# Merging three branches by tokens instead of by features, in a decoder block on one Trainium2 core

## The chip, the core and the metric

The kernel runs on one core of one Trainium2 chip. A core has a matrix engine (TensorE, PE in the profile; its weight loads are listed apart as PEld), a vector engine (DVE), a scalar engine (ACT), GpSimd (POOL) and a queue that issues transfers (SP). Each engine works through its own list of instructions in order; engines wait for each other by semaphores. SBUF is the working memory with 128 partitions, PSUM the small memory into which PE writes its sums: eight banks of 512 float32 for each partition.

The metric is the time of one execution on the device in microseconds (us). Three runs of the kernel before took 562.88, 562.93 and 563.34 us; the median is 562.93.

## What is computed

One decoder block for 256 tokens of width 1024, in float32: a sandwich of RMS norms around three token mixers that run in parallel (a sparse attention "NSA" with 16 heads in 4 groups, an mLSTM with 4 heads, cross-attention to 256 memory tokens), a merge of the three by gates, an output projection with residual, and a SwiGLU channel mixer of width 2816. The part that matters here:

```python
gm = jax.nn.sigmoid(g_merge.reshape(B, S, N_BRANCH, D_MODEL))
y = (gm[:, :, 0] * (y_nsa @ w_proj_nsa[l]) + gm[:, :, 1] * (y_ml @ w_proj_ml[l])
     + gm[:, :, 2] * (y_mem @ w_proj_mem[l]))
x = x + rmsnorm(y @ w_out[l], g_post_mix[l])
h = rmsnorm(x, g_pre_ffn[l])
gu = h @ w_ffn_in[l]
```

`g_merge` is the last part, 3 x 1024 columns, of `z = h @ w_in`. `y_nsa` has 1024 features, `y_ml` and `y_mem` have 512 each.

## The kernel before

**Exact products.** A float32 operand is split in two float32r tiles, high and low part: ACT copies (rounds) into the high one, DVE subtracts it from the source into the low one (`split`, line 429). A product is then three matmuls: high x high, high x low, low x high (`mm3`, line 457). A matmul has a stationary operand of 128 x 128, and streams up to 512 columns of the other one.

**Weights.** All large weights come as a stream of 162 units of [128, 1024] float32 (512 KB), in the order in which they are used. `unit` (line 452) fetches the next one by a DMA on SP's queue into one of four `raw` buffers and splits it into `whi` and `wlo` (four buffers each); these are ACT's `whi<-raw` and DVE's `wlo<-raw,whi` of the profile.

**Two layouts of a product.** `fmaj` (line 462) makes 128 output features for 256 tokens: the weights are stationary, the 256 tokens stream by, 24 matmuls of 256 columns for a unit of 8 blocks. `fpair` (line 470) makes two such feature tiles side by side in one PSUM bank. `tmaj` (line 477) makes [128 tokens, 512 features] for both halves of the tokens, in two banks: the activations are stationary, 512 columns of the weights stream by, 12 matmuls of 512 columns for a unit, six for each token half. In the names of the profile both look alike, for instance `pd<-hh,whi` (by features, 256 columns) and `pd<-whi,hh` (by tokens, 512).

**PSUM.** Eight banks by tags: `d` 2 (dense products, `pd`), `s` 3 (scores; `pss`, `pnl`, `sc`), `t` 2 (transposes and small things), `v` 1 (attention values). `ps_ds` (line 418) takes two of five tiles from `d` and three from `s`, in turn.

**The plan.** The program is first recorded (`Plan.record`): every instruction with what it reads and writes. `schedule` (line 265) then runs a list schedule with modelled costs: on each engine the ready instruction that comes first in the program is next. Tiles of a tag get their buffers in program order, so that a tile waits until those recorded before it have theirs. `cost` (line 228) is the model; for a matmul it is the columns divided by 2.4 per ns, plus 2 ns. The order that comes out is what the engines get.

**The stages around the change.** The attention of NSA runs over four groups `g` and two token halves `tb` (`nsa_queries`, `nsa_half`). Its chain of scores, maximum, exponential, transposes and values is long, and other work is recorded between its parts: a string `ORDER` of tasks, of which `FILL` (line 28) takes so many after each half. The first twelve tasks are parts of the mLSTM (`q`, `s`, `g`, `v`, `h`, `f`), the others are `merge_pair` ("m"): one pair of the 24 feature tiles of the merge gates, copied raw into `gm[b]` of [128, 8, 256]. `gm` has features on the partitions, one tile for each branch.

After the last group comes the merge, a loop over 8 feature tiles: the projections of the mLSTM (`pl_`), the memory branch (`pm_`) and NSA (`pn_`) by `fmaj` from two units, three multiplies with the gates, two adds (`mrg`), and a split into `yh`, `yl`. The gates' sigmoids are taken in place, after the last exponentials (`after=last_exp`), so that ACT's table is changed only once. `yh` and `yl`, features on the partitions, are the stationary operands of the output projection (`scaled`, `tmaj` by tokens with `ps_ds`), whose sums are normed and added to the residual. The channel mixer then takes the last 190 us.

Of the kernel before, what the change touches and what calls it, by code (L numbers as in the profile page):

```python
# [10 lines left out]
F32 = mybir.dt.float32  # L11
F32R = mybir.dt.float32r
# [5 lines left out]
P = 128  # L18
S = 256          # tokens
D = 1024  # L20
KD = D // P      # feature tiles of the model dimension
# [6 lines left out]
FILL = (5, 7, 1, 2, 3, 1, 3, 2)  # L28
ORDER = "qqvqqsghhhhfmmmmmmmmmmmm"
# [3 lines left out]
# columns of w_in  # L33
C_Q, C_KV, C_G, C_ML, C_IF, C_O, C_QM, C_MG = 0, 1024, 2560, 2608, 4144, 4152, 4664, 5176

# columns of the array of constants
K_ID, K_TRI, K_RV, K_BM, K_M0, K_C1, K_MT, K_END = 0, 128, 256, 257, 261, 533, 549, 677
# columns of the array of gains and small weights
# [4 lines left out]
class View:  # L43
    """A part of a tile that has no place yet."""
# [54 lines left out]
    def region(self):  # L99
        """First and last partition, and the elements of a partition as bits."""  # L100
        t = self.tile
        key = repr(self.steps)
        if key not in t.regions:
            p = int(self.ix.flat[0]) // t.n
            bits = np.zeros(t.n, bool)
            bits[self.ix[0].ravel() % t.n] = True
            t.regions[key] = (p, p + self.shape[0], int.from_bytes(np.packbits(bits).tobytes(), "big"))
        return t.regions[key]


class Slot:
    """A tile of the plan: its place is chosen when its first instruction is issued."""
# [50 lines left out]
class Plan:  # L163
    """Records the instructions in program order, with what they read and write, and issues them
    in the order of a list schedule: on every engine the ready one that comes first in the
    program. Tiles of a tag get their buffers in program order."""
# [9 lines left out]
    def later(self, n):  # L176
        """The instructions inside come as if n places later in the program."""
# [50 lines left out]
    def cost(op):  # L228
# [7 lines left out]
        if op.eng == "PE":  # L236
# [3 lines left out]
            return n / rate + 2  # L240
# [24 lines left out]
    def schedule(self):  # L265
# [10 lines left out]
        def offer(op):  # L276
            """Makes op a candidate if its new tiles can have places; else it waits for the tag."""
# [10 lines left out]
        def held(op):  # L288
            """A bank of PSUM serves one engine at a time, and so do the ports that GpSimd shares."""
# [96 lines left out]
def block_kernel(ctx, tc, order, xN, xT, memT, cst, vec, row, wg, w1, w2, W, out):  # L386
# [75 lines left out]
    def fmaj(out, xs, ks, wu, b0=0, first=True, last=True):  # L462
        """out [128 features, 256] += blocks of a unit (from b0) times the tiles ks of xs."""
# [6 lines left out]
    def fpair(xs, w, i, ps_new=ps_d):  # L470
        """[128, 2, 256]: the i-th pair of feature tiles of the weights w."""
# [5 lines left out]
    def tmaj(xs, *key, n=4, ps_new=ps_d, into=None, last=0):  # L477
        """[128 tokens, 512] for both halves of the tokens, from n units of two feature tiles each; the
        last ones are used for the first half of the tokens before the second."""
# [29 lines left out]
    def warm_up(n):  # L509
        """Products of no use, that bring the tensor engine's clock up while it would wait."""  # L510
# [4 lines left out]
    def colsum(sq):  # L515
        """[128, 2]: per token, the sum of sq [128, 2, 256] over the partitions and the tiles."""
# [7 lines left out]
    def bcast(r, ps):  # L524
        """ps [128, 256]: the column r [128, 2] of the tokens, on every row."""
# [114 lines left out]
    msk = one.tile([P, 416], BF16, name="msk")          # m0 (272), c1 (16), mt (128)  # L640
# [56 lines left out]
    # running sums of logf, and i - sums  # L697
# [34 lines left out]
    # columns: selected keys 128-255, 0-127, compressed keys, window keys 0-127, 128-255  # L732
# [63 lines left out]
    for h2 in range(2):  # L796
        pvm = ps_v([P, 2, S], "pvm")
        ptm = [[work.tile([P, 2, S], F32R, tag=f"pT{i}", bufs=2, name="pTm") for i in range(2)] for _ in range(2)]
        for tb in range(2):
# [18 lines left out]
            pt = ps_t([P, 2, 2, P], "ptx")          # m tile, head, t  # L818
# [102 lines left out]
    gm = [bigt("G", 3, [P, 8, S], F32, f"gm{b}") for b in range(3)]  # L921

    def merge_pair(i):
        ps = fpair(X, "g_merge", i)
        ACT.activation(gm[i // 4][:, 2 * (i % 4):2 * (i % 4) + 2, :], ps, AF.Copy)
# [20 lines left out]
    def nsa_half(g, tb, qs, yT):  # L946
# [71 lines left out]
        for e in range(2):  # L1018
# [5 lines left out]
             "h": ml_head, "f": lambda _: ml_finish(), "m": merge_pair}  # L1024
# [16 lines left out]
    last_exp = exps[-12:]  # L1041

    def sigmoids(i):
        for b in range(3):
            g2 = gm[b][:, 2 * i:2 * i + 2, :]
            ACT.activation(g2, g2, AF.Sigmoid, after=last_exp)
# [3 lines left out]
    for fi in range(8):  # L1050
        ps = ps_s([P, 2, S], "pnl")
        pn_, pl_, pm_ = ps[:, 0, :], ps[:, 1, :], ps_t([P, S], "pmm")
        if fi % 2 == 0:
            sigmoids(fi // 2)
        w = unit(("proj", 2 * fi + 1))
        fmaj(pl_, yml, range(4), w)
# [221 lines left out]
```

## Time and profile before

| | |
|---|---|
| median of three runs | 562.93 us |
| span of the profiled execution | 561.4 us |
| attention with tasks between, from the first scores | about 111 to 298 us |
| projections of the branches and merge | 296 to 342 us |
| output projection and residual | 342 to 391 us |
| channel mixer | to the end |
| weight stream | 159 units of 512 KB and 6 half units, 51.5% of the DMA engines' time |

The span is that of one profiled execution, from its first to its last instruction; the page gives no other time of that execution. The profile shows an instruction of PE with a modelled end. PE overlaps the end of one matmul with the next: a 256-wide one is drawn some 0.28 us long and the next begins after 0.12 us. Line numbers do not help to tell instructions apart, since the plan issues all from line 382; the names of the tiles do.

### The profile page before, as it was taken

To read this page: it belongs to the slowest core of one execution; us is meant where nothing else is said; L and a number is where in the kernel's file an instruction comes from. 1 tells how busy PE (TensorE), PEld (TensorE's weight loads), DVE (VectorE), ACT (ScalarE), POOL (GpSimd) and SP (SyncE) were. 2 spreads that over 40 slices of the span, in tenths; PEclk is the share of its full clock that TensorE was granted. 3 is DMA by queue.
4 is the path that set the end of the run, shared out by engine and by line. 5 is a ranking of instruction groups with operands and counts; after the bars stand their busy time and mean duration, and the time that the engine had idled before them with its cause. 6 is when DMAs were issued, how large, how long until landed. Compare 5 with 4: busy or idle time off the path is not lost.

```text
span 561.4 us, 10304 instructions
## 1 busy us (share of the span) xinstructions
PE 551.9 (98%) x3964; PEld 516.5 (92%) x3964; DVE 404.5 (72%) x802; ACT 334.2 (60%) x658; POOL 36.0 (6%) x44
## 2 busy tenths in 40 slices
PE   8999999999999999999999999999999999999994
PEld 8899998998989999999999998878999999988883
DVE  4897398598897989987786877865565656654543
ACT  6775677566596858777697444774444444444430
POOL 1110000002002011302111000000000000000000
PEclk9999999999999999999999999999999999999998
DMA  7994327617345253434435655744555545556522
GB/s 246 356 350 154 113 86 228 205 56 238 129 121 180 76 178 124 135 119 160 151 117 158 216 189 188 257 156 123 177 189 183 182 175 179 186 185 191 189 71 75
DMA packets 29281, 95.28 MB, mean 170 GB/s; under 512 B 3376, under 2 KB 6704, under 8 KB 28976
## 3 DMA queue, kind: packets, MB, share of 16 engines
q1 hardware_dynamic: 29232, 94.63, 51.5%
q8 instruction: 31, 0.51, 0.4%
q14 instruction: 18, 0.15, 0.1%
HBM read 92.52 MB, written 1.05 MB: 167 GB/s over the span
## 4 chain that ended last, share of the span: by engine, by line
PE 92%; DMA 3%; ACT 2%; DVE 2%; issue 0%; SPq 0%; DVEq 0%; ACTq 0%
PE pd L382 46%; PE pss L382 23%; PE pnl L382 6%; PE sc L382 3%; PE pvn L382 3%; PE pmm L382 2%; PE ptn L382 2%; DMA memt<-in_memT 2%; PE ph L382 2%; ACT whi L382 1%; DMA raw<-in_W 1%; PE pw L382 1%; PE pn L382 1%; PE pgf L382 1%; PE psm L382 1%; PE pvm L382 1%
## 5 line engine op out<-in xcount | busy, mean ns | idle before, releaser
L382 DVE TENSOR_TENSOR wlo<-raw,whi 128x1024 fp32r<-128x1024 f32 (+1 forms) x161 | 195.4, 1217 | 102.1 <-ACT whi L382 100.7
L382 ACT ACTIVATE whi<-raw 128x1024 fp32r<-128x1024 f32 (+1 forms) x161 | 167.6, 1046 | 164.3 <-issue 72.3
L382 PE MATMUL pd<-hh,whi 128*128 128x256 f32 x416 | 119.7, 288 | 0.3 <-DVE vs L382 0.3
L382 PE MATMUL pd<-hh,wlo 128*128 128x256 f32 x416 | 119.7, 288 | 0.0
L382 PE MATMUL pd<-hl,whi 128*128 128x256 f32 x416 | 119.5, 287 | 0.0
L382 PEld LDWEIGHTS pd<-hh,whi 128*128 128x128 f32 x416 | 79.5, 191 | 0.8 <-DVE vs L382 0.7
L382 PEld LDWEIGHTS pd<-hl,whi 128*128 128x128 f32 x416 | 79.4, 191 | 0.1
L382 PEld LDWEIGHTS pd<-hh,wlo 128*128 128x128 f32 x416 | 79.4, 191 | 0.0
L382 PE MATMUL pss<-xh,wlo 128*128 128x256 f32 x160 | 45.4, 284 | 0.0
L382 PE MATMUL pss<-xl,whi 128*128 128x256 f32 x160 | 45.4, 284 | 0.0
L382 PE MATMUL pss<-xh,whi 128*128 128x256 f32 x160 | 45.4, 283 | 0.0
L382 PE MATMUL pss<-whi,u 128*128 128x512 f32 x132 | 42.4, 392 | 0.0
L382 PE MATMUL pd<-xh,whi 128*128 128x256 f32 x128 | 36.2, 283 | 0.0
L382 PE MATMUL pd<-xl,whi 128*128 128x256 f32 x128 | 36.2, 283 | 0.0
L382 PE MATMUL pd<-xh,wlo 128*128 128x256 f32 x128 | 36.2, 283 | 0.0
L382 PEld LDWEIGHTS pss<-xh,whi 128*128 128x128 f32 x160 | 30.7, 192 | 0.0
L382 PEld LDWEIGHTS pss<-xl,whi 128*128 128x128 f32 x160 | 30.7, 192 | 0.0
L382 PEld LDWEIGHTS pss<-xh,wlo 128*128 128x128 f32 x160 | 30.7, 192 | 0.0
L382 PEld LDWEIGHTS pss<-whi,u 128*128 128x128 f32 x132 | 24.8, 188 | 5.5
L382 ACT ACTIVATE pp<-sc,mx 128x128 f32<-128x128 f32 (+1 forms) x64 | 27.1, 439 | 0.4 <-DVE mx L382 0.3
L382 PE MATMUL pss<-wlo,u 128*128 128x512 f32 x66 | 25.9, 392 | 0.0
L382 DVE TENSOR_REDUCE mx<-sc 128x1 f32<-128x16 f32 (+2 forms) x96 | 22.6, 284 | 3.3 <-PE sc L382 3.0
(306 smaller groups left out, 1243.9 us busy)
## 6 DMA issues: line engine op xcount, KB each, us to landing
raw<-in_W SPq DMA_DIRECT2D x159, 512.0 KB, 3.4
w<-in_w SPq DMA_DIRECT2D x2, 1024.0 KB, 7.0
raw<-in_W SPq DMA_DIRECT2D x6, 256.0 KB, 5.6
xt<-in_xT SPq DMA_DIRECT2D x2, 512.0 KB, 7.6
x<-in_xN SPq DMA_DIRECT2D x2, 512.0 KB, 4.9
out<-z SPq DMA_DIRECT2D x8, 128.0 KB, 2.0
memt<-in_memT SPq DMA_DIRECT2D x6, 128.0 KB, 5.4
wgt<-in_wg SPq DMA_DIRECT2D x1, 512.0 KB, 6.3
```

Of the source, the lines that this page charges most:

```text
L382: op.ins_ = getattr(op.real, op.method)(*map(arg, op.a), **{k: arg(x) for k, x in op.kw.items()})
```

## The change

The gates and the branch projections are made by tokens. `gm[b]` becomes [128 tokens, 2, 1024]; `merge_half` makes 512 gates of a branch for all tokens from four units, six times in all, and copies them out by ACT. `ORDER` has six "m" in place of twelve, and `FILL` puts one after each of the last six attention halves. The merge becomes a loop over two halves `h` of the features: for the mLSTM, the memory branch and NSA in this order a sigmoid in place (1024 elements at once), the projections by `tmaj` in the banks of `ps_ds`, and for each half of the tokens a multiply (and an add for the second and third branch) into a [128, 1024] tile `mrg` of tag `p`, which has two buffers. Then PE transposes the sum, four tiles of 128 x 128 into one bank (`pty`), and ACT and DVE split it into `yh` and `yl`. The plan counts 13 ns in place of 2 for each float32r matmul besides its columns. The units hold other columns of the weights; there are as many as before. Comments are gone too; the diff leaves them out.

```diff
-FILL = (5, 7, 1, 2, 3, 1, 3, 2)
-ORDER = "qqvqqsghhhhfmmmmmmmmmmmm"
+FILL = (5, 7, 1, 1, 1, 1, 1, 1)
+ORDER = "qqvqqsghhhhfmmmmmm"
...
-            return n / rate + 2
+            return n / rate + (13 if dtype == F32R and op.method != "transpose" else 2)
...
-    gm = [bigt("G", 3, [P, 8, S], F32, f"gm{b}") for b in range(3)]
-
-    def merge_pair(i):
-        ps = fpair(X, "g_merge", i)
-        ACT.activation(gm[i // 4][:, 2 * (i % 4):2 * (i % 4) + 2, :], ps, AF.Copy)
+    gm = [bigt("G", 3, [P, 2, D], F32, f"gm{b}") for b in range(3)]
+
+    def merge_half(i):
+        b, h = i % 3, i // 3
+        for tb, ps in enumerate(tmaj(X, "g_merge", b, h)):
+            ACT.activation(gm[b][:, tb, 512 * h:512 * h + 512], ps, AF.Copy)
...
-             "h": ml_head, "f": lambda _: ml_finish(), "m": merge_pair}
+             "h": ml_head, "f": lambda _: ml_finish(), "m": merge_half}
...
     last_exp = exps[-12:]
-
-    def sigmoids(i):
-        for b in range(3):
-            g2 = gm[b][:, 2 * i:2 * i + 2, :]
-            ACT.activation(g2, g2, AF.Sigmoid, after=last_exp)
 
     yh = bigt("hh", 1, [P, 8, S], F32R, "yh")
     yl = bigt("hl", 1, [P, 8, S], F32R, "yl")
-    for fi in range(8):
-        ps = ps_s([P, 2, S], "pnl")
-        pn_, pl_, pm_ = ps[:, 0, :], ps[:, 1, :], ps_t([P, S], "pmm")
-        if fi % 2 == 0:
-            sigmoids(fi // 2)
-        w = unit(("proj", 2 * fi + 1))
-        fmaj(pl_, yml, range(4), w)
-        fmaj(pm_, ymem, range(4), w, 4)
-        fmaj(pn_, (ynh, ynl), range(8), unit(("proj", 2 * fi)))
-        m = work.tile([P, 3, S], F32, tag="p", bufs=2, name="mrg")
-        for b, x in enumerate((pn_, pl_, pm_)):
-            DVE.tensor_mul(m[:, b, :], x, gm[b][:, fi, :])
-        for b in (1, 2):
-            DVE.tensor_add(m[:, 0, :], m[:, 0, :], m[:, b, :])
-        split(yh[:, fi, :], yl[:, fi, :], m[:, 0, :])
+    for h in range(2):
+        c = slice(512 * h, 512 * h + 512)
+        m = [work.tile([P, 1024], F32, tag="p", bufs=2, name="mrg") for _ in range(2)]
+        for b, name, xs, n in ((1, "proj_ml", yml, 2), (2, "proj_mem", ymem, 2), (0, "proj_nsa", (ynh, ynl), 4)):
+            g2 = gm[b][:, :, c]
+            ACT.activation(g2, g2, AF.Sigmoid, after=last_exp)
+            for tb, ps in enumerate(tmaj(xs, name, h, n=n, ps_new=ps_ds)):
+                acc, new = m[tb][:, 0:512], m[tb][:, 512:1024]
+                if b == 1:
+                    DVE.tensor_mul(acc, ps, gm[b][:, tb, c])
+                else:
+                    DVE.tensor_mul(new, ps, gm[b][:, tb, c])
+                    DVE.tensor_add(acc, acc, new)
+        for tb in range(2):
+            pt = ps_t([P, 4, P], "pty")
+            for j in range(4):
+                PE.transpose(pt[:, j, :], m[tb][:, j * P:(j + 1) * P], ident)
+            t = slice(tb * P, (tb + 1) * P)
+            split(yh[:, 4 * h:4 * h + 4, t], yl[:, 4 * h:4 * h + 4, t], pt)
...
-    add_f("g_merge", w_in, tiles(C_MG, 24))
-    pn, pl, pm = a["w_proj_nsa"][0], a["w_proj_ml"][0], a["w_proj_mem"][0]
-    for i in range(8):
-        c = slice(i * P, (i + 1) * P)
-        units["proj", 2 * i] = blocks(pn, c).reshape(P, 1024)
-        units["proj", 2 * i + 1] = np.concatenate([blocks(pl, c), blocks(pm, c)], axis=1).reshape(P, 1024)
+    for b in range(3):
+        for h in range(2):
+            c = C_MG + 1024 * b + 512 * h
+            add_t("g_merge", w_in[:, c:c + 512], b, h)
     for h in range(2):
+        for b in ("nsa", "ml", "mem"):
+            add_t("proj_" + b, a["w_proj_" + b][0][:, 512 * h:512 * h + 512], h)
```

## The prediction, made before the changed kernel was run

> **What bounds the kernel now.** I read the page first: the busy table, the 40 slices and the chain that ended last.
>
> ```profile
> span 561.4 us, 10304 instructions
> PE 551.9 (98%) x3964; PEld 516.5 (92%) x3964; DVE 404.5 (72%) x802; ACT 334.2 (60%) x658; POOL 36.0 (6%) x44
> PE   8999999999999999999999999999999999999994
> PEclk9999999999999999999999999999999999999998
> PE 92%; DMA 3%; ACT 2%; DVE 2%; issue 0%; SPq 0%; DVEq 0%; ACTq 0%
> ```
>
> TensorE (PE) is busy in every slice but the first and the last, at full granted clock, and makes 92% of the chain. Busy time of pipelined matmuls proves little, so the next view is the busy time by stretches (columns: stretch, length, then PE with its count, weight loads, DVE, ACT, POOL, clock, DMA share, GB/s). I cut it at the stages: heads and selected attention with the merge gates' products between (100 to 293), branch projections (293 to 343), output projection (343 to 395).
>
> ```profile
> 60.00:100.00 40.00, 40.00 (x298) 37.98 (x297) 31.55 (x69) 28.47 (x59) 1.31 (x1) 1.00 0.50 148
> 100.00:135.00 35.00, 34.67 (x240) 31.37 (x238) 28.89 (x70) 20.17 (x49) 5.32 (x4) 1.00 0.47 147
> 135.00:195.00 60.00, 59.88 (x449) 55.30 (x450) 51.79 (x118) 46.83 (x112) 3.13 (x3) 1.00 0.44 141
> 195.00:293.00 98.00, 98.00 (x824) 95.89 (x823) 83.04 (x227) 71.63 (x194) 14.88 (x12) 1.00 0.43 141
> 293.00:343.00 50.00, 50.00 (x418) 49.91 (x417) 39.42 (x67) 26.38 (x37) 3.49 (x2) 1.00 0.57 180
> 343.00:366.00 23.00, 22.84 (x105) 18.77 (x105) 18.18 (x24) 15.04 (x25) 0.55 (x1) 1.00 0.70 233
> ```
>
> In the two stages that the change rewrites (195 to 343) PE never shows a gap, while DVE and ACT keep room. The same holds outside: from 60 to 366 PE's idle time adds up to 0.33 + 0.12 + 0.16 = 0.61 us. So what a changed instruction is worth there is what it holds PE, from start to start, and not the duration that its row shows. The starts come from the chain of waits in order of time (start, length, what, count):
>
> ```profile
> 305.24 4.31 PE pnl L382 x36
> 309.55 1.43 PE pmm L382 x12
> 395.73 11.52 PE pd L382 x96
> 543.50 5.44 PE pss L382 x24
> 548.94 5.45 PE pd L382 x24
> ```
>
> A 256-wide product in an unbroken run takes 11.52/96 = 120.0 ns; in the projections (4.31 + 1.43)/48 = 119.6 ns. A 512-wide product (548.94, the last projection) takes 5.45/24 = 227.1 ns. Two narrow ones cost 240, one wide one 227 for the same columns: 12.9 ns saved for each pair.
>
> **The change part by part.** *Gates.* `merge_pair` ran 12 times with 2 units of 8 x 3 narrow products, 576 x 120.0 ns = 69.1 us. `merge_half` runs 6 times with 4 units x 2 token halves x 2 x 3 wide ones, 288 x 227.1 = 65.4 us. That is 3.7 us off PE. Weights, their splits and their DMAs (24 units) are the same in number.
>
> *Projections.* Before, 8 rounds of 48 narrow products, 384 x 119.6 = 45.9 us; after, two halves of 24 + 24 + 48 wide ones, 192 x 227.1 = 43.6 us: 2.3 us off PE, again with the same 16 units.
>
> The rule that speaks against these two terms is in the Trainium skill, page "TensorE: Matmul & The Clock Gate", section "Back-to-back issue gap": an isolated warm product takes one column per cycle of 2.4 GHz and 2.5 ns on top, 109 ns at 256 columns and 216 at 512. By that rule a pair saves only 2.5 ns and 480 pairs save 1.2 us. The trace does not agree (120.0 and 227.1 in fp32r runs at clock 1.00), so the sum goes by the rows.
>
> *Transposes back to features.* New are 2 x 2 x 4 = 16 transposes of 128x128 float32. The attention's own have the same shape:
>
> ```profile
> 155.39 0.66 PE ptn L382 x6
> L382 ACT ACTIVATE pTh<-ptn x24: 575/596/667, 119.6 to 290.8; 128x512 fp32r<-128x512 f32 x24
> L382 DVE TENSOR_TENSOR pTl<-ptn,pTh x24: 640/682/692, 120.3 to 291.5; 128x512 fp32r<-128x512 f32 x24
> ```
>
> 0.66/6 = 110 ns each, 16 x 110 = 1.8 us onto PE. On the bound engine the sum so far is -3.7 - 2.3 + 1.8 = -4.2 us.
>
> *DVE and ACT* get less work:
>
> ```profile
> L382 ACT ACTIVATE gm<-gm 128x512 f32<-128x512 f32 x12 | 6.8, 620 | 0.0
> L382 DVE TENSOR_TENSOR mrg<-mrg 128x256 f32<-128x256 f32 x16 | 6.7, 421 | 0.2
> L382 DVE TENSOR_TENSOR mrg<-pnl,gm 128x256 f32<-128x256 f32 x16 | 6.0, 420 | 3.2 <-PE pnl L382 3.2
> L382 DVE TENSOR_TENSOR wlo<-raw,whi 128x512 fp32r<-128x512 f32 x6 | 4.1, 689 | 1.7 <-ACT whi L382 1.7
> ```
>
> DVE had 40 multiplies and adds of 256 at 0.42 = 16.8 us; it gets 20 of 512, at 0.69 by the nearest row of that width, 13.8 us. The final splits go from 8 of 256 to 4 of 512. None of this is on PE's path, so I cost it at nothing; the cover is PE's stream (DVE 39.42 of 50 us from 293 to 343), and without that cover it would be a gain.
>
> *Handing over the banks of tag `d`.* A pair of feature tiles took one of the two banks, and its copy out had a whole pair (48 x 120 ns = 5.8 us) to happen in. A merge half takes both, its two token halves end six wide products (1.36 us) apart, and whatever wants a `d` bank next (the next half, or the next group's queries, which stand behind it in the tag's order) waits for the copy. The kernel has three such uses already; one of them shows what a handover costs:
>
> ```profile
> 100.91 0.39 PE L382 MATMUL pd<-whi,hl 128*128 128x512 f32 x1
> 101.33 0.60 ACT L382 ACTIVATE vs<-pd 128x512 fp32r<-128x512 f32 x1 [0.76 <-PE pd L382]
> 101.59 0.39 PE L382 MATMUL pd<-hh,whi 128*128 128x256 f32 x1 [0.29 <-DVE vs L382]
> L382 ACT ACTIVATE gm<-pd 128x512 f32<-128x512 f32 x12 | 7.1, 591 | 0.2 <-PE pd L382 0.2
> ```
>
> From 100.91 to 101.59 are 0.68 us where a wide product holds PE 0.23: a hole of 0.45. There DVE had to read the bank after ACT (0.60, then 0.68); a merge half's copy is ACT's 0.59 alone, 0.42 us after the last start by that same row, so the first bank is free about 1.0 us after its last product starts, inside the 1.36. The bounds are 0 and 6 x 0.45 = 2.7 us; a split (about 1.05) ahead of the copy on ACT would spoil it now and then, so I take 0.1 each, 0.6 us.
>
> *The end of the merge.* The sum of the second half of the features must go through DVE, PE, ACT and DVE before the output projection's third unit can start (its first two need only the first half of the features). Step by step for the last token half: 0.42 from the last start to the multiply (row at 101.33), 0.69 multiply, 0.69 add, four transposes 0.44 and about 0.2 to their end, 0.60 and 0.68 for the split, and about 0.3 from ACT to DVE, some 4.1 us with the small steps. The cover is two units for both token halves, 24 x 227 ns = 5.45 us. DVE also splits weights in that time:
>
> ```profile
> L382 DVE TENSOR_TENSOR wlo<-raw,whi 128x1024 fp32r<-128x1024 f32 x155 | 191.2, 1238 | 100.4 <-ACT whi L382 99.0 <-PE ptn L382 0.7
> ```
>
> With one of these (1.2) in its way the chain just fits, with two it sticks out by 1.2 us. I take 0.3 between 0 and 1.2.
>
> *The start of the merge* becomes easier. The projections of the mLSTM and the memory branch for the first half of the features come first, 48 x 227 ns = 10.9 us that need nothing from the last attention group; before, two such blocks (24 x 120 ns = 2.9 us) stood ahead of the first product that did, and that sufficed without a gap. No term.
>
> *FILL and the planner's 13 ns.* Between the queries of groups 1, 2 and 3 and the merge stood 3, 4 and 5 pairs, now 4, 4 and 4 pairs' worth. The higher count per product takes the plan's narrow product from 108.7 to 119.7 ns, the measured spacing. Both only reorder. The gain is bounded by the 0.61 us of visible idle time above (holes under 0.16 us do not show, because a narrow row is drawn 0.28 long); for a loss I take the same size. Value 0.
>
> Sum: -4.2 + 0.6 + 0.3 = -3.3 us on the profiled span of 561.4, 558.1. The median of the runs, 562.93, lies 1.5 us above that span; nothing of the change touches what lies around it. Forecast **559.6 us**, with 558.0 to 561.2 as its own range (no hole at all and 0.6 better order: -4.8; handovers at 0.3 each and the end at 1.0: -1.4).
>
> **The rivals.** *Handovers bite (slower).* If each merge half leaves a hole of 1.0 us, as when two ACT splits stand ahead of the copy, six of them are 6.0: 561.4 - 4.2 + 6.0 + 0.3 + 1.5 = 565.0. It decides from 0.65 us per half ((4.2 - 0.3)/6). For it: ACT is 73% busy in that stage (71.63 of 98), the next group's queries stand behind both banks, and the `vs` row is such a hole. Against it: other attention products and the first token half of the next units can run in the meantime, the worst hole seen was 0.45 with a longer copy, and PE waits for ACT nowhere long.
>
> *The gain is eaten (no change).* All handovers at 0.45 and the end of the merge at its 1.2: -4.2 + 2.7 + 1.2 = -0.3, 562.6. For it: both prices are in the rows. Against: all must fall to the bad side.
>
> *A wide product saves too little (the change does not do what it says).* Where two narrow products cost no more than a wide one, as would be if the 12.9 ns were a matter of those two stages' operands, the 480 pairs save nothing and the transposes' 1.8 and the holes' 0.9 are left: 561.4 + 2.7 + 1.5 = 565.6. Break-even is 2.7 us/480 = 5.6 ns per pair. For it speaks only that wide products between attention products, where most of the new ones go, are not in the rows above; against it, that the narrow spacing is the same in two stages with different operands, and that the wide one follows from `pss` (5.44/24) as from `pd`. By the rule of the Trainium skill named above (2.5 ns a pair) this case would come out at about 564.4; the trace bears it out nowhere.
>
> **How the numbers follow.** Forecast 0.74 (with a better order included), handovers bite 0.12, gain eaten 0.11, too little per product 0.03. Measurement tells 0.2% (1.1 us) from no change. Faster than 561.8 takes all of the forecast and a little of the third case: 0.77. Within 0.2%: 0.10. Slower: 0.13. The range runs from 557.4 (0.6 below the forecast's own, for holes that the rows hide) to 563.0, so that the gain eaten is in it and most of the two slower cases are out.
>
> **What would show it.** Right: the products of the gates and projections at 227 ns from start to start, 480 of them in place of 960, PE's visible idle time still under 1 us between 60 and 366, the output projection starting 4 to 5 us earlier and the stages behind it of equal length. The handover term is wrong if the copies into `gm` carry long waits and the next product on `pd` starts over 0.65 us late. The end term is wrong if the third unit of the output projection waits for `yl`. The whole is wrong if PE shows gaps in the attention stage, which would mean that the attention's chains, and not PE, set its length, or if stages that the change does not touch grow.

## The result: slower, and the profile after

The changed kernel takes 568.49 us (median of 4 runs, 567.64 to 569.74) against 563.13 us (the three runs of the kernel before named above and a fourth, 563.34): ratio 1.0093, 95% interval 1.0076 to 1.0109. The forecast was 559.6, the range 557.4 to 563.0.

From the page of the changed kernel: span, busy table, two rows of the 40 slices, and the chain that ended last.

```profile
span 566.8 us, 9365 instructions
PE 553.4 (98%) x3500; PEld 491.0 (87%) x3500; DVE 402.5 (71%) x778; ACT 333.9 (59%) x648; POOL 36.9 (7%) x44
PE   8999999999999999999999999899999999999995
PEclk9999999999999999999999999989999999999999
PE 83%; DVE 6%; ACT 6%; DMA 2%; issue 2%; SPq 1%; DVEq 0%; ACTq 0%
```

PE is still "98% busy", but its share of the chain went from 92% to 83%: DVE and ACT now end waits that PE ended before. Slice 26 shows less PE and slice 27 a lower clock (a slice is 14.2 us, so this is about 354 to 383), a first hint of one place. The stretches of the changed kernel (columns as before):

```profile
195.00:293.00 98.00, 97.49 (x601) 82.14 (x600) 81.94 (x227) 70.93 (x190) 14.65 (x11) 1.00 0.41 146
366.00:395.00 29.00, 26.63 (x121) 21.51 (x119) 15.22 (x32) 15.91 (x32) 1.26 (x2) 0.94 0.34 115
370.00:375.00 5.00, 5.00 (x15) 4.01 (x16) 4.32 (x11) 2.38 (x7) 0.56 (x1) 0.68 0.55 180
```

Most of the stretch from 366 belongs to a stage that the change does not touch. To see all stages at once I took, for every run, the start of the first matmul of each stage in its profile; the columns are lengths in us. "Attention" runs from the first scores to the first product of the branch projections, "norm" from the output projection's last product to the first product of the channel mixer after its first gate unit and first up unit, "rest" to the last product. (A column is a difference of two starts, so it needs no modelled ends. Each row is one execution. After, e3 and e5 have the same order of products up to the output projection: there the attention is 184.9 in all three, but the time to the first scores 112.5, 112.7 and 114.0, so differences of a us in that column say little.)

| kernel | time | to first scores | attention | merge | output projection | norm, first units | rest |
|---|---|---|---|---|---|---|---|
| before | 563.13 | 111.3 | 184.8 | 46.2 | 21.6 | 25.0 | 165.1 |
| after | 568.49 | 112.5 | 184.9 | 45.4 | 22.4 | 29.1 | 165.1 |
| after, count of 2 ns (e1) | 562.23 | 110.8 | 181.6 | 45.3 | 22.4 | 27.9 | 165.1 |
| before, count of 13 ns (e2) | 572.16 | 113.5 | 190.5 | 45.9 | 21.6 | 26.5 | 165.1 |
| e1 and turn reset (e4) | 560.5 | 111.3 | 181.7 | 45.3 | 22.4 | 26.0 | 165.1 |
| e4 and true exponentials (e15) | 558.6 | 111.3 | 180.3 | 45.3 | 22.4 | 25.2 | 165.1 |

The two rewritten stages gained nothing in the first and 0.8 us in the second, and the norm behind them lost 4.1. The rows of e1 and e2 split this at once.

### The profile page after: what moved, and what is told of

The parts are those of the page before. It is cut to its first block, busy times and chain, and to the rows that moved or that the text cites. A ratio compares the mean times of both kernels' runs of the same rounds, so it can differ in the third digit from the quotient of the medians.

```text
span 566.8 us, 9365 instructions
## 1 busy us (share of the span) xinstructions
PE 553.4 (98%) x3500; PEld 491.0 (87%) x3500; DVE 402.5 (71%) x778; ACT 333.9 (59%) x648; POOL 36.9 (7%) x44
## 4 chain that ended last, share of the span: by engine, by line
PE 83%; DVE 6%; ACT 6%; DMA 2%; issue 2%; SPq 1%; DVEq 0%; ACTq 0%
PE pd L382 44%; PE pss L382 27%; PE pvn L382 3%; PE sc L382 2%; ACT whi L382 2%; PE ptn L382 2%; PE ph L382 2%; ACT pp L382 1%; DVE wlo L382 1%; DMA memt<-in_memT 1%; DMA raw<-in_W 1%; SPq L382 1%; DVE mx L382 1%; DVE wq L382 1%; DVE cm L382 1%
## 5 line engine op out<-in xcount | busy, mean ns | idle before, releaser
L382 PE MATMUL pd<-hh,whi 128*128 128x256 f32 x224 | 64.1, 286 | 0.3 <-DVE vs L382 0.3
L382 PE MATMUL pd<-hh,wlo 128*128 128x256 f32 x224 | 64.0, 286 | 0.0
L382 PE MATMUL pd<-hl,whi 128*128 128x256 f32 x224 | 63.8, 285 | 0.0
L382 PE MATMUL pd<-whi,hh 128*128 128x512 f32 x144 | 57.8, 404 | 0.0
L382 PE MATMUL pd<-wlo,hh 128*128 128x512 f32 x144 | 57.7, 401 | 0.0
L382 PE MATMUL pd<-whi,hl 128*128 128x512 f32 x144 | 57.5, 400 | 0.0
L382 PEld LDWEIGHTS pd<-hh,whi 128*128 128x128 f32 x224 | 42.9, 192 | 1.0 <-DVE vs L382 0.7
L382 PEld LDWEIGHTS pd<-hl,whi 128*128 128x128 f32 x224 | 42.8, 191 | 0.2
L382 PEld LDWEIGHTS pd<-hh,wlo 128*128 128x128 f32 x224 | 42.8, 191 | 0.0
L382 PEld LDWEIGHTS pd<-whi,hh 128*128 128x128 f32 x144 | 27.2, 189 | 4.4 <-issue 0.2
```

The lines of the kernel that those rows point to most:

```text
L382: op.ins_ = getattr(op.real, op.method)(*map(arg, op.a), **{k: arg(x) for k, x in op.kw.items()})
```

## The experiments

A ratio is always to the kernel before on the same chip, with its 95% interval. The letters of the theories are those of the expectation they stand in.

### The change in its two parts

*e1: the changed kernel with the old count.*

```diff
-            return n / rate + (13 if dtype == F32R and op.method != "transpose" else 2)
+            return n / rate + 2
```

> The changed kernel with the plan's old cost of a matmul (2 ns in place of 13 besides its columns); the order on ACT then has two weight splits ahead of the split of the normed residual (xh), as before, and not three. Theory A (the order that the new cost makes is what loses the time): the 2.3 us hole before gate0's first product and the cold clock behind it go, the stage from the last product of the output projection to the first of ffn_in falls from 29.0 to about 25 us, and the time to 564 or less. Theory B (the new layout loses it: transfers come late behind the faster merge): the stage stays near 29 us and the time at 568.5.

562.23 us, 0.9991 (0.9979 to 1.0003): below the 564 of theory A, though the norm stage is still 27.9 and not 25. *e2: the kernel before with the new count alone*, the same line the other way round.

> The kernel before with the new cost of 13 ns alone, nothing else; its order on ACT has three weight splits ahead of xh. Theory A: the hole before gate0 and the cold clock appear without any change of the merge, +4 us, about 567. Theory B: same time as before, 563.

572.16 us, 1.0171 (1.0149 to 1.0192): more than twice the loss that theory A gave, and elsewhere. The attention is 5.7 longer and the time to the first scores 2.2; the norm is only 1.5 longer, without a cold clock. The one line in the planner's model costs 6.3 us with the new layout (562.23 to 568.49; 5.9 if each is taken against its own runs of the kernel before) and 9.4 us with the old one (562.75 to 572.16). The layout by itself brings 0.9 us on the profile's span (561.4 to 560.5), which the ratio does not tell from nothing: 3.2 in the attention, 0.9 in the merge, and 0.5 before the first scores, against 0.9 in the output projection and 3.0 in the norm.

Where the 13 ns cost time in the attention shows in what the weight loads of PE waited for from 195 to 293 us (columns: engine, tile, what it waited for, us in total, times, longest). The kernel before:

```profile
PEld sc L382 <- ACT pp L382: 0.3, 2, 0.2
```

The changed kernel:

```profile
PEld sc L382 <- ACT pp L382: 2.7, 8, 0.6
PEld pvn L382 <- ACT pTh L382: 1.0, 2, 0.7
PEld ptn L382 <- DVE pp L382: 0.4, 2, 0.2
```

and the changed kernel with the old count (e1), whose attention is 3.3 us shorter:

```profile
PEld pvn L382 <- ACT pTh L382: 0.8, 2, 0.4
PEld sc L382 <- ACT pp L382: 0.7, 2, 0.4
PEld ptn L382 <- DVE pp L382: 0.3, 1, 0.3
```

PE reaches the next scores before ACT has taken the exponentials (`pp`) out of the bank. Part of such a wait lies under the product that still runs and part under the tail with which it is drawn, so the busy time of the same stretch shows 0.51 us of idleness (98.00 - 97.49) where the three rows of the changed kernel add up to 4.1. A look at PE's idle time would have missed the 3.3 us by which the stage is longer than in e1.

### The norm behind the output projection

Two things come together there. ACT's timeline in the kernel before (start, length, line, operation, idle time before it in brackets):

```profile
361.42 1.07 ACT L382 ACTIVATE whi<-raw 128x1024 fp32r<-128x1024 f32 x1 [0.89 <-DMA raw<-in_W]
362.92 1.06 ACT L382 ACTIVATE whi<-raw 128x1024 fp32r<-128x1024 f32 x1 [0.44 <-DMA raw<-in_W]
363.89 1.04 ACT L382 ACTIVATE sq<-x 128x1024 f32<-128x1024 f32 x1
364.93 2.16 ACT L382 ACTIVATE xh<-ptx,vc 128x128 fp32r<-128x128 f32 x8
```

and in the changed kernel:

```profile
362.52 1.06 ACT L382 ACTIVATE whi<-raw 128x1024 fp32r<-128x1024 f32 x1 [0.91 <-DMA raw<-in_W]
365.13 1.06 ACT L382 ACTIVATE whi<-raw 128x1024 fp32r<-128x1024 f32 x1 [1.56 <-DMA raw<-in_W]
366.39 1.06 ACT L382 ACTIVATE whi<-raw 128x1024 fp32r<-128x1024 f32 x1 [0.20 <-DMA raw<-in_W]
367.35 1.04 ACT L382 ACTIVATE sq<-x 128x1024 f32<-128x1024 f32 x1
368.39 0.86 ACT L382 ACTIVATE xh<-ptx,vc 128x128 fp32r<-128x128 f32 x3
```

The plan puts three weight splits ahead of `xh` (the operand of the next product) instead of two, and each waits for its transfer, up to 1.56 us. ACT works in order, so `xh` stands behind a DMA that has nothing to do with it. PE in the changed kernel:

```profile
365.60 1.34 PE L382 MATMUL ptx<-cs,x 128*128 128x128 f32 x8
368.79 0.73 PE L382 MATMUL pss<-wq,xh 128*128 128x512 f32 x2 [1.86 <-ACT xh L382]
...
370.55 1.05 PE L382 MATMUL pss<-wq,xh 128*128 128x512 f32 x2
371.40 0.63 PE L382 MATMUL pss<-wq,xl 128*128 128x512 f32 x1
371.83 1.05 PE L382 MATMUL pss<-wq,xh 128*128 128x512 f32 x2
372.68 0.63 PE L382 MATMUL pss<-wq,xl 128*128 128x512 f32 x1
373.11 0.69 PE L382 MATMUL pss<-wq,xh 128*128 128x512 f32 x2
```

A wait of 1.86 us, and then a second bill: the six products from 370.55 to 373.11 take 2.56 us, 427 ns each instead of 227, in the stretch (370 to 375) in which the granted clock is 0.68. That is 6 x 0.2 = 1.2 us for the clock alone.

*e3: the changed kernel with the splits of the `ffn_up` units 1 to 3 and the sum of squares held back behind the first token half's `xh`* (an `after=` in the plan; nothing is computed otherwise).

```diff
+    late.update({("ffn_up", u): tuple(xhs[:8]) for u in (1, 2, 3)})
...
-        ACT.activation(sq, x1[:, tb, :], AF.Square, accum_out=sf[:, tb:tb + 1])
+        ACT.activation(sq, x1[:, tb, :], AF.Square, accum_out=sf[:, tb:tb + 1], after=tuple(xhs[:8]))
```

> The changed kernel with its new cost, but the plan must place ACT's splits of the second to fourth unit of ffn_up, and the sum of squares of the residual, behind the first token half's xh. Theory A: this hole alone is mended, -2.3 us of hole and about -2 of cold clock, 564 to 565; what is left over the kernel before's 563 lies ahead of the output projection. Theory B: xh is not what gate0 waits for in the end (a later transfer is), so less than 1 us is won.

566.75 us, 1.0068 (1.0044 to 1.0093), above the 564 to 565 that were expected; the norm stage falls from 29.1 to 26.0, and no product in it runs at half clock. So the order on ACT makes up all that the 13 ns cost there (1.2 against e1's 27.9), and the clock's share with it.

*e4: what the layout itself costs in the norm.* In e1, with the old count, the stage is still 27.9 instead of 25.0. Its PE timeline:

```profile
360.40 1.03 PE L382 MATMUL ptx<-cs,x 128*128 128x128 f32 x8
362.76 0.73 PE L382 MATMUL pss<-wq,xh 128*128 128x512 f32 x2 [1.33 <-ACT xh L382]
...
369.15 1.32 PE L382 MATMUL ptx<-cs,x 128*128 128x128 f32 x8
371.25 0.72 PE L382 MATMUL pss<-wq,xh 128*128 128x512 f32 x2 [0.78 <-ACT xh L382]
371.81 0.39 PE L382 MATMUL pss<-whi,xh 128*128 128x512 f32 x1
```

Twice eight transposes, twice a hole, and the first product of the up unit (`whi`) comes only after the second. The reason is in `ps_ds`, which gives two of five tiles from tag `d` and three from `s`, in turn. The new merge takes its 12 tiles from it, 12 modulo 5 is 2, so all later tiles move by two places: the first gate unit's tiles come from `s`, `s` instead of `d`, `d`, and the first tile of the up unit, also from `s`, gets its bank in program order only after the gate's second one, which waits for the second `xh`. e4 resets the turn:

```diff
+    turn[0] = 0
     for tb, r in scaled("w_out", (yh, yl), 4, g1, z, (1.0 / D, 1.0 / D), (1.0, 1.0)):
```

> The changed kernel with the old cost (2 ns), and the turn of ps_ds set back to 0 before the output projection, so that its banks and those of gate0 and up0 are those of the kernel before (d s s s, d d, s s). Theory C (the merge's twelve tiles shift the turn by two, gate0 falls into tag s, and up0's first tile, behind gate0's second in that tag's order, cannot fill the wait for the second token half's xh): the stage from the last product of the output projection to the first of ffn_in falls from 27.9 us (e1) to about 25, the hole of 1.2 us behind the second transposes goes, and the time is 562.2 - 3 = 559.3, clearly faster than before. Theory D (weights come late there because the stage before it got shorter, whatever the banks): no change against e1, 562.

560.5 us, 0.995 (0.9936 to 0.9964), the norm stage 26.0: theory C, short of its 559.3 and 25. Its PE timeline:

```profile
363.24 0.74 PE L382 MATMUL pd<-wq,xh 128*128 128x512 f32 x2 [1.25 <-ACT xh L382]
363.82 0.40 PE L382 MATMUL pss<-whi,xh 128*128 128x512 f32 x1
...
369.56 0.39 PE L382 MATMUL pss<-whi,xl 128*128 128x512 f32 x1
...
370.71 0.60 PE L382 MATMUL ptx<-cs,x 128*128 128x128 f32 x4
```

The gate is back on `pd`, and products of the up unit stand where the second hole was. The first wait (1.25) remains, since two splits still stand ahead of `xh`. *e5* is e4 with the 13 ns, *e6* is e4 with the order of e3.

> The changed kernel with its cost of 13 ns and the turn set back to 0 before the output projection. Theory C: about 2 us less than the changed kernel, 566.5, the three weight splits ahead of xh and the attention's holes stay. Theory D: 568.5.

567.44 us, 1.008 (1.006 to 1.0101): the reset brings 1.1 us here by the medians, which the intervals do not separate from nothing, and the count still costs 6.9.

> The kernel of e4 (old cost, turn set back) with ACT's splits of the second to fourth unit of ffn_up and the residual's sum of squares placed behind the first xh. If the 1.4 us hole that e4 still has before gate0 is ACT standing in a split that waits for its transfer, ahead of xh, the stage from the last product of the output projection to ffn_in falls from 26.0 to about 24.9 and the time from 560.5 to 559.3. If the late sum of squares then holds up gate0's silu instead, no gain, 560.5.

560.47 us, 0.9954 (0.9941 to 0.9966): a miss. The wait for `xh` falls from 1.25 to 0.22 us, but the stage gets only 0.5 us shorter, and the medians do not show it.

### The price of a pair, in place

*e9: e4 with every product of the gates and projections cut into two of 256 columns*, all else as it was.

```diff
+                for q in range(parts_):
+                    o = slice(q * 512 // parts_, (q + 1) * 512 // parts_)
...
+                    PE.matmul(ps[tb][:, o], xs[0][:, k, t], hi[:, w], start=(k == 0 and q == 0), stop=False, **kw)
```

> The kernel of e4 with each 512-wide product of the gates and the projections made as two of 256 columns with the same stationary operand: same layout, same banks, 480 more products. If a wide product saves 12.9 ns over two narrow ones also between attention products, these two stages get 3.7 and 2.5 us longer and the time is 566.5. If it saves next to nothing there, 561.

564.76 us, 1.0026 (1.0015 to 1.0037): 4.3 us more than e4, 8.9 ns for each of the 480 pairs. The same block in the chain of waits (start, length, count), e4:

```profile
304.71 10.89 PE pd L382 x48
```

and e9:

```profile
307.49 11.52 PE pd L382 x96
```

226.9 ns for a wide product and 120.0 for a narrow one: in an unbroken run of the new merge the pair costs 13.1 ns too. The rule of the Trainium skill (page "TensorE: Matmul & The Clock Gate", section "Back-to-back issue gap") for isolated products, which makes 2.5 ns a pair, is not what these runs show. The whole comes to 4.3 and not 6.2 us (480 x 12.9 ns): e9 loses 2.7 of 3.7 us in the attention and 2.1 of 2.5 in the merge, and its norm is 0.8 shorter than e4's. That some of the longer products fill time in which PE would have waited is likely, but not shown.

### Why a truer count makes a worse order

The 119.7 ns that the plan now takes for a narrow product is what the profile shows. Yet both kernels lose. *e7 and e11 go the other way, a count of -9 ns*, before and in e4.

```diff
-            return n / rate + 2
+            return n / rate - (9 if dtype == F32R and op.method != "transpose" else -2)
```

> The kernel before with the cost of a float32r matmul 11 ns lower than it was (9 ns less than its columns). Theory A1 (a plan that thinks PE faster than it is puts more independent products ahead of each dependent one, and this margin is what keeps PE fed): the attention stage from the first scores to the first branch projection stays at 185 us or less, time 562 to 564. Theory A2 (any change of the cost away from the one that the order was chosen with loses some us by chance): 566 or more, like the 13 ns.

> The kernel of e4 with a cost 11 ns lower still (9 ns under the columns). Theory A1: more margin than the old cost does not hurt the attention stage, 181.7 us or a little less, time within 1 us of e4's 560.5. Theory A2 (each cost but the tuned one loses by chance): 564 or more.

563.59 us, 1.0005 (0.9995 to 1.0015), and 563.0 us, 0.9994 (0.9976 to 1.0011). The attention stage is hardly harmed by too small a count (185.3, against 184.8; 181.7, as in e4), while 13 ns lengthen it by 3 to 6 us. So in the attention it is no matter of a lucky order that any move destroys. At the norm it may be: e11 lost 1.7 there, and its time missed the 561.5 of theory A1. *e8 and e10 keep the 13 ns and count all of ACT and DVE a tenth higher*, before and in e5.

```diff
-            return (50 if psum else 95) + 0.833 * n + 93 * ("accum_out" in op.kw or pointers > 0)
+            return 1.1 * ((50 if psum else 95) + 0.833 * n + 93 * ("accum_out" in op.kw or pointers > 0))
...
-            return 67 + (0.52 if fast else 1.04) * n + 60 * pointers
+            return 1.1 * (67 + (0.52 if fast else 1.04) * n + 60 * pointers)
```

> The kernel before with the new cost of 13 ns for matmuls, and all costs of ACT and DVE times 1.1 as well, so that the ratio of PE to them is about the old one; latencies and transfers as they were. Theory A1: most of the 9.4 us that the 13 ns cost the kernel before comes back, 563 to 566. Theory A2: no return, 570 or more.

> The changed kernel with its 13 ns, the turn set back, and the costs of ACT and DVE times 1.1: the ratio of PE to the others as in e4. Theory A1 (the margin): the attention stage falls from 184.9 to about 182 us, the split ahead of xh goes, time 560.5 to 562.5 against e5's 567.4. Theory A2 (chance): 566 or more.

567.02 us, 1.007 (1.0056 to 1.0083), the attention back from 190.5 to 186.1; and 565.12 us, 1.0029 (1.0011 to 1.0046), back from 184.9 to 182.6. Both times lie between what the two theories gave. *e12, e5 with 100 ns more latency from ACT and from DVE to other engines*, asks for a fixed margin instead.

```diff
-    LAT = {"PE": 257.0, "ACT": 202.0, "DVE": 188.0, "POOL": 75.0, "SP": 980.0}
+    LAT = {"PE": 257.0, "ACT": 302.0, "DVE": 288.0, "POOL": 75.0, "SP": 980.0}
```

> The changed kernel with its 13 ns and the turn set back, and 100 ns added to the latencies that the plan counts behind ACT and behind DVE to another engine: margin put where the waits are, with PE's cost at its measured size. Theory A1: the attention stage falls from 184.9 (e5) to about 182 us; the three splits ahead of xh stay, so the norm stage stays near 28 us; time 564 to 565 against e5's 567.4. If margin on latencies does not do what the cheaper product did, 567.

566.09 us, 1.0043 (1.0028 to 1.0058), the attention only 184.3: a margin of this size at the handovers brings back 0.6 us of the 3.2. That points to something on ACT or DVE that lasts longer than the plan counts. ACT in the attention of the changed kernel:

```profile
239.82 0.27 ACT L382 ACTIVATE pc<-sc,mx 128x16 f32<-128x16 f32 x1
239.98 0.20 ACT L382 ACTIVATION_READ_ACCUMULATOR pc<-sc,mx 128x1 f32 x1
240.07 0.47 ACT L382 ACTIVATE pp<-sc,mx 128x256 f32<-128x256 f32 x1
240.43 0.21 ACT L382 ACTIVATION_READ_ACCUMULATOR pp<-sc,mx 128x1 f32 x1
240.52 0.48 ACT L382 ACTIVATE pp<-sc,mx 128x256 f32<-128x256 f32 x1
```

One exponential is two instructions: the function, and the readout of its sum. From start to start the 256-wide one takes 0.45 us (240.07 to 240.52), of which the readout holds the last 0.09, and the 16-wide one 0.25 (239.82 to 240.07). The plan counts 50 + 0.833 x 256 + 93 = 356 and 156 ns, 94 too few each: its 93 ns stand for a pointer *or* an accumulated sum, and these have both. The groups of ACT's instructions count them (out<-in, count, then busy time and mean ns of one):

```profile
L382 ACT ACTIVATION_READ_ACCUMULATOR pp<-sc,mx 128x1 f32 x64 | 14.0, 219 | 0.0
L382 ACT ACTIVATION_READ_ACCUMULATOR pc<-sc,mx 128x1 f32 x32 | 6.8, 212 | 0.0
```

96 exponentials with 94 ns each are 9 us of ACT that the plan did not see. The theory was: two errors of one direction, PE too fast and the exponentials too fast, that cancelled; the change mended one. *e13 (on e5), e14 (on e2) and e15 (on e4) mend the other.*

```diff
-            return (50 if psum else 95) + 0.833 * n + 93 * ("accum_out" in op.kw or pointers > 0)
+            return (50 if psum else 95) + 0.833 * n + 93 * (("accum_out" in op.kw) + (pointers > 0))
```

> The changed kernel with the turn of the score banks reset at the output projection and 13 ns (567.4 us, attention stage 184.9 from the first scores to the first branch projection), and in the plan 93 ns more for every activation that carries an accumulated sum. The trace shows these exponentials 0.34, 0.25 and 0.45 us from start to start for 128, 16 and 256 columns, where the plan counts 0.25, 0.16 and 0.36. Theory A (the old, too fast count for the matmuls made up for these too cheap exponentials, so that mending the one alone spoiled the order): attention 182.0 to 182.8, the waits of pv's products on pp back under 2 us, time about 565, since the three splits ahead of xh at the norm remain. Theory B (the order at 13 ns is bad for another reason, such as the proportion of TensorE to all work of VectorE and ScalarE): attention 184.5 or more, 567 to 568.

565.43 us, 1.0044 (1.0027 to 1.0061), attention 182.5.

> The kernel before with 13 ns (572.16 us, attention stage 190.6) and the same 93 ns more for each accumulating activation. Theory A: attention 185 to 187, time 567 to 568. Theory B: attention 190 or more, 571.5 to 572.5.

568.67 us, 1.0085 (1.0051 to 1.0119), attention 187.9: theory A's direction, though 0.9 us short of its numbers in the stage. The profiled execution lost the clock there: from 140 to 144 us 0.57 is granted, and 15 products of 256 columns take 3.2 us (140.38 to 143.59) instead of 1.8. Without these 1.4 us the stage would be at 186.5, as theory A had it.

> The best version so far (changed kernel, count of 2 ns, turn reset: 560.5 us, attention 181.7) with the same 93 ns more for each accumulating activation. Theory A: the attention stage stays at 181.7 or gains some tenths, 560.0 to 560.8; nothing is lost, since the waits that the plan underrates grow shorter or were hidden. Theory B says nothing sure of it; a loss of over 1 us, as when the count is lowered to -9 (563.0), would say that any move of the plan's counts costs and that their truth has little to do with it.

558.6 us, 0.9914 (0.9902 to 0.9927), attention 180.3: the best version of all, 1.9 us below e4 and better than expected. From 195 to 293 us no wait of PE's weight loads is listed at all, nor is one in e13.

What is left of the 13 ns in the attention is 2.2 us (182.5 in e13, 180.3 in e15), and the trace shows most of it as one hole. PE and ACT in e13:

```profile
138.40 0.35 PE L382 MATMUL pd<-hh,whi 128*128 128x256 f32 x1 [1.75 <-DVE vml L382]
134.27 1.05 ACT L382 ACTIVATE whi<-raw 128x1024 fp32r<-128x1024 f32 x1
135.22 0.58 ACT L382 ACTIVATE vml<-pd 128x512 fp32r<-128x512 f32 x1
```

and ACT in e15, where PE has no listed wait there:

```profile
133.97 0.59 ACT L382 ACTIVATE vml<-pd 128x512 fp32r<-128x512 f32 x1
134.45 1.06 ACT L382 ACTIVATE whi<-raw 128x1024 fp32r<-128x1024 f32 x1
```

With 13 ns ACT has a weight split ahead of its copy out of a bank of tag `d` (the values of the mLSTM, `vml`), DVE's part comes later with it, and the next product on `pd` waits 1.75 us. e14 and e16 have the same order and the same 1.75. It is the mechanism of the rival "handovers bite", at a use of the banks that the layout did not touch.

*e16: e13 with the order of e3 at the norm; e17: the kernel before with the true exponentials alone.*

> The changed kernel at 13 ns with all three mends found: the turn of the score banks reset, the true count of the accumulating exponentials, and the splits of the later weight units placed behind the first token half's xh (565.43 us without the last of them; its stage from the output projection's last product to the first product of the rest of the feed-forward block is 28.2 us). If what 13 ns costs there is the order of ScalarE alone: that stage 25.2 to 25.8, time 562.4 to 563.2, and what is left against the best version (558.6) is 1.2 before the first scores and 2.2 in the attention. If it is not: 28 and 565.

562.62 us, 0.9993 (0.9976 to 1.001). The norm stage is 25.5 instead of e13's 28.2 (which had 3.4 us at half clock, from 366.5), and over that stage the granted clock is 1.00:

```profile
363.00:388.00 25.00, 24.57 (x116) 19.93 (x116) 14.67 (x30) 15.75 (x32) 1.26 (x2) 1.00 0.39 126
```

So at the norm the order of ACT, with the clock that its wait costs, is all but 0.3 us of it (e15: 25.2).

> The kernel before at its own count of the matmuls, with the 93 ns more for each accumulating activation alone (562.93 to 563.4 us; attention stage 184.8). If the true count of these exponentials helps by itself, as with the changed layout (1.9 us, 1.45 of them in the attention stage): attention 183.3 to 184.0, time 561.3 to 562.5. If the gain of the best version hangs on its layout: 563.0 to 563.8.

561.61 us, 0.997 (0.9956 to 0.9983), attention 182.8 instead of 184.8. The mended count helps the old layout as well; it is no matter of the new one. It also limits the theory of e13: if the two errors had cancelled, mending the exponentials alone would have cost time. It gains at either count, in the new layout 1.4 us of attention at 2 ns and 2.5 at 13. So only some 1.0 of the 3.2 us between e4 and e5 can be the missing counterweight; the truer count of the matmuls loses with true exponentials too.

## Why the prediction was wrong

**The failing step is "FILL and the planner's 13 ns": "Both only reorder … Value 0."** The planner's 13 ns measured +6.3 us (e1 to after), ten times the bound of 0.61; FILL was not tried alone. The bound was wrong on both sides. It does not even limit what a better order can gain: e17 gives the kernel before another order and nothing else, and its attention is 2.0 us shorter, the time 1.5. From the first scores to the merge the weight loads of the kernel before wait 1.3 us for `pp`, which its visible idle time does not show and which e17 does not have. And nothing limits what a worse order can lose; taking "the same size" for the loss had no ground. By stages the 6.3 us of the span are 1.7 before the first scores, 3.3 in the attention and 1.2 in the norm (with 0.1 in the merge). The prediction did see that 119.7 ns is the measured spacing; that a truer figure may make the plan worse was not considered. A look at the exponentials' start-to-start distances against the plan's formula, both at hand, would have raised the doubt.

**A missing term: the turn of the score banks.** `ps_ds` in the new merge was in the diff; what its 12 tiles do to the turn of all later tiles was not followed. e1 to e4: 1.7 us by the medians, 1.9 in the norm stage. Of the 3.0 that the layout costs there, the remaining 1.1 fits the first wait for `xh` (1.25 in e4's row, 0.16 in the kernel before), though e6 shortens that wait to 0.22 and the stage by half as much only; e15's stage is 0.2 longer than that of the kernel before (25.2 to 25.0), with a wait of 0.36.

**The products were right in an unbroken run, and too large in place.** The profile has 464 matmuls fewer (3964 to 3500): 480 products less and 16 transposes more, as forecast. The forecast for the gates was -3.7, with +0.6 for the handovers -3.1 in the attention; e1 measured -3.2. That agreement is in part luck: no handover cost is seen (below), and by e9 the wide gates are worth 2.7 in the attention, not 3.7, so the rest of the 3.2 is probably order. For projections and transposes it was -2.3 + 1.8 + 0.3 = -0.2 over merge and output projection together; e1 measured -0.9 and +0.9, about nothing. (The second half's transposes run inside the output projection, hence the split.) The output projection starts at 337.72 in e1, 4.6 us earlier than the 342.35 before: within the "4 to 5 us" that would show it. Two slips in the working change nothing: by its own terms the forecast's range ends at 561.5, not 561.2, and two weight splits let the end of the merge stick out by some 1.1 us, not 1.2.

**The handovers cost nothing to be seen.** All copies of the gates in e1, by what ACT did before them:

```profile
L382 ACT ACTIVATE gm<-pd x12: 597/600/667, 190.1 to 292.9; 128x512 f32<-128x512 f32 x12
...
  PE pd L382: 3.4, 6
```

ACT waited for PE, six times; no wait of PE for a copy is listed in e1. Nor is one for the end of the merge (0.3 in the sum): from 296 to 361 us PE and its weight loads have no listed wait there. "Handovers bite" (0.12) is refuted for the merge halves, as are "the gain is eaten" by these prices and "a wide product saves too little": in place a pair saves 8.9 ns (e9), above the break-even of 5.6. The sum for the layout was -3.3; without the missing bank term (e4) it measured -2.6, 560.5 against 563.08.

**The sign of what would prove it wrong was named**, "if stages that the change does not touch grow": the norm did, by 4.1 us: 1.9 by the turn of the banks (e4), 1.2 by the count (e1 to after), and 1.0 that the layout alone leaves, with the first wait for `xh`. The other sign named, gaps of PE in the attention, came too, though more in the waits of the weight loads than in the idle time.

**Open.** With the exponentials counted truly, the 13 ns still cost 2.2 us in the attention, 1.75 of it in the hole at `vml`, and 4.0 in all between e16 and e15 by the medians (562.62 and 558.6; 3.0 by the spans), though e16 also has the norm's order mended. With the old layout it is 7.1 between e14 and e17 (568.67 and 561.61). Why the plan puts the split ahead of that copy was not sought. Whether another count is too small, or a list schedule simply does better when it thinks PE faster than it is and so keeps work queued ahead of PE, was not settled: e7 and e11 (too fast by more, no gain and hardly a loss in the attention) fit the second, but do not show it. The lengths before the first scores, 110.8 to 111.4 with a count of 2 or -9 and 111.8 to 114.0 with 13, rise with the count; the cause of that was not sought. (e10's 116.0 has 6.8 us at half clock in it, from 48 us on: the granted clock is 0.55 from 48 to 52 and 0.60 from 52 to 56.)

## What to carry to other kernels

A cost model in a planner is a change of every stage at once: value its edit by the stages it can disturb, not by the idle time it could remove. A truer count is no better order by itself: on the kernel before, the matmuls' truer count alone gave 1.0171, the exponentials' alone 0.997, both 1.0085, and in the new layout with the turn reset 1.008, 0.9914 and 1.0044 against 0.995 for neither. So each count is worth a run of its own. Where tiles come from pools in turn, a stage that takes a number of them that isn't a multiple of the turn shifts the banks of everything behind it; one reset line was worth 1.7 us at a count of 2 ns. An in-order engine that splits weights as they arrive must not have a late transfer ahead of the one operand that PE waits for.

## What the hardware showed

A hole of less than 2 us can cost the clock: PE waited 1.86 us before 368.79, and the products from 370.55 to 373.11 ran at 427 ns instead of 227. In e14 the hole at `vml`, 1.75 us with no product or transpose in it, ended at 138.84, and the stretch behind it is:

```profile
140.00:144.00 4.00, 4.00 (x23) 4.00 (x22) 0.84 (x3) 1.80 (x5) 0.00 (x0) 0.57 0.48 150
```

Behind the same 1.75 us in e13 and e16 the granted clock is 1.00 (140 to 195), so the length of a wait alone does not decide. At the norm it fell behind 1.63 us in e5 and 1.55 in e13. After the 1.33 us in e1 (at 362.76) the clock stayed up, by the stretch that follows:

```profile
364.00:369.00 5.00, 5.00 (x22) 3.97 (x22) 4.67 (x11) 2.98 (x6) 0.55 (x1) 1.00 0.40 138
```

The Trainium skill (page "TensorE: Matmul & The Clock Gate", section "Wait — 56ns, not 53.3ns?") gives 426.7 ns from start to start for 512 columns on a cold array; the trace agrees with its 427. PE's visible idle time in the kernel before adds up to 0.61 us between 60 and 366, so the price of a cold clock was in none of the terms.

And the sum of an exponential is not free on ACT: the profile lists its readout as an instruction of its own, `ACTIVATION_READ_ACCUMULATOR`, and the next instruction starts 0.09 us after it does (240.43 to 240.52), which is the 94 ns that the plan did not count.
